# The input projection u @ w_in by Strassen's algorithm, ahead of the merges

## The chip, the cores and the metric

The kernel runs on one core of one Trainium2 chip. The metric is the device time of one launch in microseconds (us). Engines are named as the profile names them: PE (TensorE, matrix products), PEld (its weight loads), DVE (VectorE), ACT (ScalarE), POOL (GpSimd) and SP (SyncE, which here only issues DMAs). Each engine takes its instructions strictly in order; semaphores tie the engines together.

## What is computed

One layer with 1024 tokens and 1024 channels, in float32, cut to what matters:

```python
u = layer_norm(x) * (1 + scale) + shift              # shift, scale, gate from silu(c) @ w_ada + b_ada
proj = u @ w_in + b_in                               # w_in: 1024 x 12288
a_v, a_g, b_b, b_c, b_h, b_g, c_a, c_b, c_g, merge = split(proj)   # 1024 each, merge 3 x 1024
y_a = grouped_linear(causal_pool(a_v), pool_w) * pool_scale * silu(a_g)   # windows 2, 4, 8, 16
y_b = b_b * causal_dwconv3(b_c * b_h) * silu(b_g)
h_c = causal_dwconv31(c_a * sigmoid(c_b))
y_c = silu(layer_norm(h_c)) * silu(c_g)
m = sum_k sigmoid(merge_k) * (y_k @ w_branch[k])
out = layer_norm(ALPHA * x + gate * (m @ w_out))
```

## The kernel before

Channels lie on the 128 partitions and tokens on the free dimension, so blocks of weights are the stationary operand. float32 products are made of float32r parts: each operand is split into a high part (ACT, L97) and a low part (DVE subtracts, L98), and each product goes through PE in three passes (`mm3`, L100 to L103): low weights by high data, high by low, high by high.

The work is a list of jobs (`Job`, L260). A *projection job* takes one block of 128 columns of w_in: it loads 512 KB of raw weights on SP's queue, splits them in two pieces of 512, runs 8 k x 2 halves of the tokens x 3 passes = 48 matmuls of 128x512 into one PSUM tile of 1024 tokens, and then a function given to `proj` (L312) takes the result out of PSUM with its bias. There are 96 of them. A *z job* does the same with a column block of w_branch and the y of one branch (24 jobs); four *pool jobs* hold the grouped linear map. Loads are issued two jobs ahead, splits one job ahead.

The branches: `c_pair` (L345) makes the input of the 31-tap convolution, `conv_step` (L364) runs TAPS = 4 of its taps on DVE after each job, `a_v`, `a_g`, `a_pool` are branch A, `b_tile` branch B (four projections), the `c_` functions from L490 the layer norm of branch C. `merge` (L565) alternates a gate (a projection job with a sigmoid) and a z job, so all gates stay in SBUF only shortly, and y0, y1, y2 are kept split in SBUF. The convolution's outputs go to DRAM (h_dram) and come back (hc).

A hand-written list, START, sets the order of the first 80 us: statistics of x, the modulation sums, transposes, the pieces of u (`ul`, `uh`) and the products of the first three jobs as the pieces arrive. After that the jobs run in the order of the list, and a scheduler places each engine's instructions. Buffers: a pool of 44 tiles of 128 x 1024 (4 KB per partition) for everything large, two raw weight buffers, four buffers for split weights of 512 columns, and three PSUM tiles of 1024.

Of the kernel before, what the change touches and what calls it, by code (L numbers as in the profile page):

```python
# [35 lines left out]
BIG_SLOTS = 44  # L36
RAW_BUFS = 2
SPLIT_BUFS = 4
TAPS = 4
OUT_PARTS = (2, 2, 2, 2, 2, 2, 2, 4)  # L40
PAIR_EVERY = 6
C_STAGE = 4
C_YS = (0, 1, 2, 2, 3, 3, 4, 4)
# [5 lines left out]
def kernel(  # L49
# [26 lines left out]
    def main_ps(name):  # L76
        return ps_main.tile([P, D], F32, tag="main", name=name)
# [9 lines left out]
    def after(late, early):  # L87
        """Keeps the scheduler from issuing a load, and taking its slot, ahead of time."""
# [11 lines left out]
    def mm3(ps, wh, wl, rh, rl, start, stop):  # L100
        nc.tensor.matmul(ps, wl, rh, start=start, stop=False)  # L101
        nc.tensor.matmul(ps, wh, rl, start=False, stop=False)  # L102
        nc.tensor.matmul(ps, wh, rh, start=False, stop=stop)  # L103

# [18 lines left out]
    def columns(name, parts, q, cols=None):  # L123
        """Vectors of DRAM, each as columns of 128 channels."""
# [22 lines left out]
    u_hi = [slot(f"uh{k}", F32R) for k in range(NT)]  # L147
    u_lo = [slot(f"ul{k}", F32R) for k in range(NT)]
# [50 lines left out]
    def ada_sum(k):  # L199
        """c_act times the rows of w_ada; partition p of each part sums the rows p of some tiles."""  # L200
# [59 lines left out]
    class Job:  # L260
# [304 lines left out]
    def merge(b, AHEAD=2):  # L565
# [27 lines left out]
        for d in range(AHEAD):  # L593
            gate(d)
# [236 lines left out]
```

## Time and profile before

| what | value |
|---|---|
| median of 3 runs | 1480.46 us (1479.98 to 1480.49) |
| span of the profiled execution | 1479.1 us |
| PE busy | 1456.3 us, 98% |
| DVE busy | 851.8 us, 58% |
| ACT busy | 361.7 us, 24% |
| POOL busy | 27.2 us, 2% |
| moved by DMA | 104.53 MB, 71 GB/s |

The profiled execution has no time of its own beside its span; the span stands 1.4 us under the median of the runs, which were taken without a profile. A row of a group reads: line, engine, operation, output<-inputs by the program's names, shapes, count, then busy us and mean ns of one, then idle time of that engine just before and what ended it. A matmul is listed with its own latency, which is longer than the distance between two, since they are pipelined.

### The profile page before, as it was taken

The page shows a single profiled execution, that of the slowest core. Times are in us where ns is not written, and L with a number is a line of the kernel's source. Part 1 is how long each engine was busy: PE and PEld are TensorE (multiplying, and loading weights), DVE is VectorE, ACT ScalarE, POOL GpSimd, SP SyncE. Part 2 cuts the span into 40 slices and gives each one's busy share as a digit, 9 for nine tenths or more (in the row PEclk, how much of TensorE's full clock was granted, in tenths as well). Part 3 has the DMA queues.
Part 4 walks back from the last instruction along what each step waited for, and adds up shares of the span by engine and source line. Part 5 has one row for each costly group of instructions (what it writes and reads, how often), then busy time and mean ns, then how long its engine had stood idle before and what let it go on. Part 6 is the DMA issues. An engine that isn't in the chain of part 4 may idle for free.

```text
span 1479.1 us, 15467 instructions
## 1 busy us (share of the span) xinstructions
PE 1456.3 (98%) x6505; PEld 1208.2 (82%) x6505; DVE 851.8 (58%) x977; ACT 361.7 (24%) x478; POOL 27.2 (2%) x63
## 2 busy tenths in 40 slices
PE   7899999999999999999999999999999999999997
PEld 6788878888888888888888888888888888888887
DVE  6669999989393764939632332312224566322676
ACT  5433222222211112121221222211112346212300
POOL 1100000000000000000000000000000000000010
PEclk9999999999999999999999999999999999999999
DMA  9513322121212111121111111211114111112422
GB/s 306 134 29 100 108 71 65 43 64 43 72 43 66 49 58 57 43 68 47 57 57 43 46 55 43 58 43 43 57 43 163 51 43 43 57 43 66 162 100 86
DMA packets 152903, 104.53 MB, mean 71 GB/s; under 512 B 3844, under 2 KB 144208, under 8 KB 152832
## 3 DMA queue, kind: packets, MB, share of 16 engines
q1 hardware_dynamic: 150992, 98.06, 22.3%
q0 software_dynamic: 1792, 5.46, 1.1%
q8 instruction: 51, 0.84, 0.2%
q14 instruction: 20, 0.16, 0.0%
q10 hardware_dynamic: 48, 0.01, 0.0%
HBM read 95.12 MB, written 8.39 MB: 70 GB/s over the span
## 4 chain that ended last, share of the span: by engine, by line
PE 96%; SPq 3%; DMA 0%; DVE 0%; issue 0%; ACT 0%; DVEq 0%
PE ps_p L102 23%; PE ps_p L103 23%; PE ps_p L101 23%; PE ps_z L101 6%; PE ps_z L102 6%; PE ps_z L103 6%; SPq L191 2%; PE out_ps L101 2%; PE out_ps L103 2%; PE out_ps L102 2%; SPq L168 1%; PE pool_ps L103 0%; PE pool_ps L102 0%; PE pool_ps L101 0%; DMA raw_p<-in_w_in_dram 0%; PE tr L240 0%
## 5 line engine op out<-in xcount | busy, mean ns | idle before, releaser
L102 PE MATMUL ps_p<-ul,w_p 128*128 128x512 f32 x1536 | 599.5, 390 | 0.4 <-DVE ul L257 0.4
L103 PE MATMUL ps_p<-uh,w_p 128*128 128x512 f32 x1536 | 599.1, 390 | 0.0
L101 PE MATMUL ps_p<-uh,w_p 128*128 128x512 f32 x1536 | 596.9, 391 | 0.2 <-DVE w_p L98 0.2
L101 PEld LDWEIGHTS ps_p<-uh,w_p 128*128 128x128 f32 x1536 | 288.6, 188 | 61.6 <-issue 0.9
L102 PEld LDWEIGHTS ps_p<-ul,w_p 128*128 128x128 f32 x1536 | 289.3, 188 | 60.7 <-DVE ul L257 0.9
L103 PEld LDWEIGHTS ps_p<-uh,w_p 128*128 128x128 f32 x1536 | 289.2, 188 | 60.1
L373 DVE SCALAR_TENSOR_TENSOR h<-cs,cfw_cols,h 128x1023 f32<-128x1023 f32 (+14 forms) x240 | 303.7, 1266 | 7.9 <-ACT h L371 4.0
L98 DVE TENSOR_TENSOR w_p<-raw_p,w_p 128x512 fp32r<-128x512 f32 x192 | 131.5, 687 | 237.0 <-ACT w_p L97 236.8
L97 ACT ACTIVATE w_p<-raw_p 128x512 fp32r<-128x512 f32 x192 | 120.3, 629 | 488.0 <-PE ps_p L103 354.1
L98 DVE TENSOR_TENSOR w_z<-raw_z,w_z 128x512 fp32r<-128x512 f32 x48 | 33.0, 688 | 78.7 <-ACT w_z L97 78.7
L97 ACT ACTIVATE w_z<-raw_z 128x512 fp32r<-128x512 f32 x48 | 30.3, 631 | 157.2 <-PE ps_z L103 129.6
L580 DVE TENSOR_TENSOR g<-ps_z,g 128x1024 f32<-128x1024 f32 x24 | 29.4, 1224 | 68.0 <-PE ps_z L103 68.0
L573 ACT ACTIVATE g<-ps_p,bin_cols 128x1024 f32<-128x1024 f32 x24 | 26.8, 1115 | 100.7 <-PE ps_p L103 100.7
L324 DVE SCALAR_TENSOR_TENSOR bg<-ps_p,bin_cols,bg 128x1024 f32<-128x1024 f32 x8 | 10.3, 1282 | 31.2 <-ACT bg L323 31.1
L459 DVE SCALAR_TENSOR_TENSOR bc<-ps_p,bin_cols,bc 128x1024 f32<-128x1024 f32 x8 | 10.3, 1284 | 24.7 <-PE ps_p L103 24.7
L474 DVE SCALAR_TENSOR_TENSOR ba<-ps_p,bin_cols,ba 128x1024 f32<-128x1024 f32 x8 | 10.3, 1284 | 22.5 <-PE ps_p L103 22.5
L467 DVE SCALAR_TENSOR_TENSOR ba<-bc,vec_cols,ba 128x1023 f32<-128x1023 f32 (+1 forms) x16 | 20.5, 1281 | 4.5 <-ACT ba L463 4.3
L781 DVE TENSOR_TENSOR og<-out_ps,gate_b 128x512 f32<-128x512 f32 (+1 forms) x18 | 11.2, 629 | 19.9 <-PE out_ps L103 19.9
L356 DVE SCALAR_TENSOR_TENSOR cs<-ps_p,bin_cols,cs 128x1024 f32<-128x1024 f32 x8 | 10.3, 1281 | 20.7 <-PE ps_p L103 20.7
L324 DVE SCALAR_TENSOR_TENSOR cg<-ps_p,bin_cols,cg 128x1024 f32<-128x1024 f32 x8 | 10.2, 1281 | 19.2 <-ACT cg L323 19.2
L584 DVE TENSOR_TENSOR g<-g,g 128x1024 f32<-128x1024 f32 x16 | 19.5, 1218 | 0.0
L228 PE MATMUL mod<-c_act,ada 128*128 128x1 f32 x64 | 14.0, 352 | 5.2 <-DMA ada<-in_w_ada_dram 5.2
(452 smaller groups left out, 1536.3 us busy)
## 6 DMA issues: line engine op xcount, KB each, us to landing
raw_p<-in_w_in_dram SPq DMA_DIRECT2D x96, 512.0 KB, 3.9
raw_z<-in_w_branch_dram SPq DMA_DIRECT2D x24, 512.0 KB, 3.6
ada<-in_w_ada_dram SPq DMA_DIRECT2D x32, 256.0 KB, 6.4
x<-in_x_dram SPq DMA_DIRECT2D x8, 512.0 KB, 6.2
rawg<-in_w_ada_dram SPq DMA_DIRECT2D x8, 512.0 KB, 3.7
h_dram<-h POOLq DMA_DIRECT2D x8, 512.0 KB, 3.3
hc<-h_dram SPq DMA_DIRECT2D x8, 512.0 KB, 6.9
rawo<-in_w_out_dram SPq DMA_DIRECT2D x8, 512.0 KB, 3.7
```

The costliest lines, as they stand in the source:

```text
L97: nc.scalar.activation(hi, src, AF.Identity)
L98: marks["split"] = nc.vector.tensor_tensor(out=lo, in0=src, in1=f32(hi), op=ALU.subtract)
L101: nc.tensor.matmul(ps, wl, rh, start=start, stop=False)
L102: nc.tensor.matmul(ps, wh, rl, start=False, stop=False)
L103: nc.tensor.matmul(ps, wh, rh, start=False, stop=stop)
L191: nc.sync.dma_start(out=t[:, s], in_=ada_src[:, s, 4 * q : 4 * q + 4, k * P : (k + 1) * P])
L324: nc.vector.scalar_tensor_tensor(out=t, in0=ps, scalar=bias(col), in1=t, op0=ALU.add, op1=ALU.mult)
L373: nc.vector.scalar_tensor_tensor(out=h[:, s:], in0=g[:, : S - s], scalar=w, in1=h[:, s:], op0=ALU.mult, op1=ALU.add,)
L467: nc.vector.scalar_tensor_tensor(out=a[:, s:], in0=g[:, : S - s], scalar=vec("sc_w", (2 - s) * NT + ct), in1=a[:, s:], op0=ALU.mult, op1=A ...
L573: marks["u_done"] = nc.scalar.activation(gates[d], ps, AF.Sigmoid, bias=bias(col))
L580: nc.vector.tensor_mul(g, ps, g)
L584: marks["z"] = nc.vector.tensor_add(m[d], m[d], g)
```

## The change

All of u @ w_in but four column blocks is computed by Strassen's algorithm in its form with seven products. w_in's rows are cut into even and odd blocks k, and two column blocks form a *pair*; u is cut likewise into even and odd blocks and into the two halves of the tokens. So a pair is a 2x2 by 2x2 product of quarters: A11, A12 (first column block, even and odd rows), A22 (second column block, odd rows) and the sums S1 to S4 on the weights' side; B11, B21, B22 and the sums T1 to T4 on u's side. Each of the seven products is 4 blocks x 3 passes = 12 matmuls of 128x512.

- `sum_u` makes the sums of u once, after the start: 16 subtractions in place on DVE (L276 to L279) and eight splits of 1024.
- `Pair.prepare` makes S1 to S4 (four DVE instructions of 512, L368 to L372) and splits wa = the first raw block, wb = S1 and S2, wc = S3 and S4 (1024 each) and wd = A22 (512).
- `Pair.run` accumulates in two PSUM banks, which are read between products (ACT, L396, L398, L400), and puts the rest together by three DVE additions (L403, L405, L407).
- The functions that follow are rewritten for pairs (`c_pair`, `a_pair`, `b_first`, `b_second`, `gates`). Gates, y1, the silus of a_g and c_g, the pooled tiles and the centred convolution are stored in DRAM by POOL's queue (`store`) and loaded again (`y_load`, `a_load`, `c_square`, `c_y`, the g of `merge`).
- All pairs come first (4 ordinary jobs, then 46 pairs); then the z jobs of branch B with the pool jobs between them, then those of A, then of C. No gate is made between z jobs.
- TAPS is 6, then 5. Big tiles 44 to 37, raw buffers 2 to 4, split buffers 3 of 1024 columns, and six PSUM banks of 512 instead of three tiles of 1024. Silu is used as one function of ACT where the kernel before used Sigmoid and a multiplication.

```diff
-BIG_SLOTS = 44
-RAW_BUFS = 2
-SPLIT_BUFS = 4
-TAPS = 4
+BIG_SLOTS = 37
+RAW_BUFS = 4
+W8_BUFS = 3
+TAPS = 6
+TAPS_LATE = 5
+CLASSIC = 4
...
+    def sum_u(i):
+        even, odd = ut[2 * i], ut[2 * i + 1]
+        b11, b12, b21, b22 = even[:, LEFT], even[:, RIGHT], odd[:, LEFT], odd[:, RIGHT]
+        nc.vector.tensor_sub(b11, b12, b11)
+        nc.vector.tensor_sub(b12, b22, b12)
+        nc.vector.tensor_sub(b22, b22, b11)
+        nc.vector.tensor_sub(b21, b21, b22)
+        for n, t in ((0, even), (1, odd)):
+            hi, lo = slot(f"t{i}_{n}h", F32R), slot(f"t{i}_{n}l", F32R)
+            split(hi, lo, t)
+            sums[i, n] = hi, lo
...
+    class Pair:
+        def prepare(self):
...
+            wa = split8(f"wa_{self.name}", raw1)
+            nc.vector.tensor_add(s1, a2[:, 0], a2[:, 1])
+            nc.vector.tensor_sub(s2, s1, a1[:, 0])
+            wb = split8(f"wb_{self.name}", s12.rearrange("p n c -> p (n c)"))
+            nc.vector.tensor_sub(s3, a1[:, 0], a2[:, 0])
+            nc.vector.tensor_sub(s4, a1[:, 1], s2)
+            wc = split8(f"wc_{self.name}", s34.rearrange("p n c -> p (n c)"))
+            wd = wlast.tile([P, 2, HALF], F32R, tag="last", name=f"wd_{self.name}")
...
+        def product(self, ps, left, right, first):
+            w, block = self.left[left]
+            for i in range(4):
+                ks = slice(block(i) * P, (block(i) + 1) * P)
+                rh, rl = quarter(right, i)
+                mm3(ps, w[:, 0, ks], w[:, 1, ks], rh, rl, first and i == 0, i == 3)
+
+        def run(self):
...
+            self.product(px, "A11", "B11", True)
+            nc.scalar.activation(r1[:, LEFT], px, AF.Identity, bias=bias(col1))
+            self.product(pz, "S1", "T1", True)
+            nc.scalar.activation(r2[:, RIGHT], pz, AF.Identity, bias=bias(col2))
+            self.product(px, "S2", "T2", False)
+            nc.scalar.activation(r1[:, RIGHT], px, AF.Identity, bias=bias(col1))
+            py = bank(f"py_{self.name}")
+            self.product(py, "A12", "B21", True)
+            nc.vector.tensor_add(r1[:, LEFT], py, r1[:, LEFT])
+            self.product(px, "S3", "T3", False)
+            nc.vector.tensor_add(r2[:, RIGHT], px, r2[:, RIGHT])
+            self.product(pz, "S4", "B22", False)
+            nc.vector.tensor_add(r1[:, RIGHT], pz, r1[:, RIGHT])
+            self.product(px, "A22", "T4", False)
+            self.after(r1, px, r2)
...
+    def func(t, ps, f, col):
+        nc.scalar.activation(t[:, LEFT], ps, f, bias=bias(col))
+        nc.scalar.activation(t[:, RIGHT], t[:, RIGHT], f)
...
+    def y_load(b, k, mark):
+        t = slot(f"y{b}_{k}")
+        after(nc.sync.dma_start(out=t, in_=y_dram[b][k]), marks[mark])
+        y[b, k] = split_slots(f"y{b}_{k}", t)
...
+    def ahead(i):
+        for n, have, f in ((i + 2, loaded, "load"), (i + 1, prepared, "prepare")):
...
+        if i == n_proj - 1:
+            for k in range(NT):
+                y_load(1, k, "late")
```

The written order shows where this puts the work. First DVE, early among the projections. Before, between the low parts of two jobs' weights (w_p6272 in two pieces, then the first of w_p384), there are taps of the convolution (L373), a sum of the gate row (L700) and branch A's work:

```order
L98 TENSOR_TENSOR w_p6272_0_1137<-raw_p6272_1055,w_p6272_0_1137 128x512
L700 SCALAR_TENSOR_TENSOR gacc_1053<-rawg1_1132,c_act_117,gacc_1053 128x1024
L373 SCALAR_TENSOR_TENSOR h0_773<-cs0_768,cfw_cols_756,h0_773 128x1007
L373 SCALAR_TENSOR_TENSOR h0_773<-cs0_768,cfw_cols_756,h0_773 128x1006
L406 TENSOR_TENSOR s2_1_1114<-v2_1112 128x1023
L98 TENSOR_TENSOR w_p6272_512_1140<-raw_p6272_1055,w_p6272_512_1140 128x512
L373 SCALAR_TENSOR_TENSOR h0_773<-cs0_768,cfw_cols_756,h0_773 128x1005
L406 TENSOR_TENSOR s2_2_1117<-s2_1_1114 128x1022
L373 SCALAR_TENSOR_TENSOR h0_773<-cs0_768,cfw_cols_756,h0_773 128x1004
L98 TENSOR_TENSOR w_p384_0_1204<-raw_p384_1135,w_p384_0_1204 128x512
```

After, in the middle of pair d2 (branch B's second pair of tile 2), with the weights of cg2 (gates of branch C) being prepared and b2 being finished:

```order
L403 TENSOR_TENSOR r1_d2_2067<-py_d2_2108,r1_d2_2067 128x512
L112 TENSOR_TENSOR wa_cg2_2049<-raw_cg2_0_1910,wa_cg2_2049 128x1024
L477 SCALAR_TENSOR_TENSOR h2_2165<-r1_c2_1674,cfw_cols_836,h2_2165 128x1019
L564 SCALAR_TENSOR_TENSOR r2_b2_1935<-r1_b2_1934,vec_cols_832,r2_b2_1935 128x1023
L407 TENSOR_TENSOR r1_d2_2067<-pz_d2_2066,r1_d2_2067 128x512
L112 TENSOR_TENSOR wb_cg2_2054<-s12_cg2_2047,wb_cg2_2054 128x1024
L477 SCALAR_TENSOR_TENSOR h2_2165<-r1_c2_1674,cfw_cols_836,h2_2165 128x1018
L405 TENSOR_TENSOR r2_d2_2068<-px_d2_2065,r2_d2_2068 128x512
L564 SCALAR_TENSOR_TENSOR r2_b2_1935<-r1_b2_1934,vec_cols_832,r2_b2_1935 128x1022
L809 SCALAR_TENSOR_TENSOR gacc_1648<-rawg4_2173,c_act_123,gacc_1648 128x1024
L112 TENSOR_TENSOR wc_cg2_2059<-s34_cg2_2048,wc_cg2_2059 128x1024
L368 TENSOR_TENSOR s12_b3_2180<-raw_b3_1_2045 128x512
```

The low parts of the weights have become 1024 wide, and between them stand the sums of quarters and the additions that read PSUM (py, pz, px).

Second SP, at the passage to a merge. Before, in the approach to the third merge, the loads of the convolution's outputs (hc) stand together between raw weights of projection jobs:

```order
L507 DMA hc0_6993<-h_dram0_136 128x1024 [waits DMASW1_49,PE_49]
L274 DMA raw_p8704_7084<-in_w_in_dram 128x8x128 [waits DMAHW0_49,DVE_49]
L507 DMA hc1_6998<-h_dram1_137 128x1024 [waits DMASW4_49,PE_49]
L507 DMA hc2_7004<-h_dram2_138 128x1024 [waits DMASW7_49,DMASW5_49,DMASW0_49]
L507 DMA hc3_7006<-h_dram3_139 128x1024 [waits DMASW6_49,PE_49]
```

After, at the first merge, raw weights of z and pool jobs stand between loads of the tiles that these same jobs read (raw weights wait for DVE, whose split frees the buffer):

```order
L674 DMA y1_7_7014<-y1_dram7_149 128x1024 [waits DMAHW0_49,PE_49]
L525 DMA pool0_7020<-pool_dram0_158 128x1024 [waits DMAHW1_49,DMASW2_49,PE_49]
L300 DMA raw_pool3_7412<-in_pool_w_dram 128x2x256 [waits DMAHW2_49,DVE_49]
L528 DMA sga0_7026<-sga_dram0_166 128x1024 [waits DMAHW3_49,PE_49]
L525 DMA pool1_7028<-pool_dram1_159 128x1024 [waits DMASW5_49,DMASW4_49,DMAHW4_49,DMASW2_49,DMASW1_49]
...
L300 DMA raw_z1_5_7558<-in_w_branch_dram 128x8x128 [waits DMAHW4_49,DVE_49]
L626 DMA hc4_7161<-h_dram4_130 128x1024 [waits DMAHW5_49]
L626 DMA hc5_7168<-h_dram5_131 128x1024 [waits DMAHW6_49]
L525 DMA pool2_7175<-pool_dram2_160 128x1024 [waits DMAHW7_49,PE_49]
```

What moved is what the jobs of a merge read: it was in SBUF as it was made, and now comes through SP's queue, behind raw weights of later jobs.

More of the change, by code (lines that the diff above doesn't have):

```diff
@@ L334, with store, dram_tiles @@
+    def store(dst, src):
+        return nc.gpsimd.dma_start(out=dst, in_=src)
+    def dram_tiles(name, n):
+        return [dram.tile([P, S], F32, name=f"{name}{j}") for j in range(n)]
+    jobs = []
     hooks = {}
@@ new lines, in y_load, with merge, done @@
+    def y_load(b, k, mark):
+        t = slot(f"y{b}_{k}")
+        after(nc.sync.dma_start(out=t, in_=y_dram[b][k]), marks[mark])
+        y[b, k] = split_slots(f"y{b}_{k}", t)
+    def merge(b, first):
+        def z(d):
+            def done(ps):
+                g = slot(f"g{b}_{d}")
+                after(nc.sync.dma_start(out=g, in_=g_dram[b][d]), marks["late"])
+                for h in range(2):
+                    nc.vector.tensor_mul(g[:, HALVES[h]], ps[h], g[:, HALVES[h]])
+                if first:
@@ L609 @@
-    merge(0)
-    for ct in range(NT):
-        b_tile(ct)
-    rest = jobs[n_first:]
-    del jobs[n_first:]
-    j = 1
-    for i, job in enumerate(rest):
-        jobs.append(job)
-        if i % PAIR_EVERY == PAIR_EVERY - 1 and j < NT:
+    for j in range(CLASSIC // 2):
+        c_classic(j)
+    todo = []
+    for j in range(NT):
+        todo.append([lambda j=j: b_first(j), lambda j=j: b_second(j)])
+    for j in range(NT):
+        todo.append([lambda j=j: a_pair(j)])
+    light = [lambda i=i: gates(f"cg{i}", C_CG + 2 * i * P, AF.Silu, sgc_dram[2 * i : 2 * i + 2]) for i in range(NT // 2)]
@@ new lines @@
+    for b in (1, 0, 2):
+        for i in range(NT // 2):
+            light.append(
+                lambda b=b, i=i: gates(
+                    f"m{b}_{i}", C_M + b * D + 2 * i * P, AF.Sigmoid, g_dram[b][2 * i : 2 * i + 2]
+                )
+            )
+    heavy = [f for group in todo for f in group]
+    heavy_n, light_n = len(heavy), len(light)
+    order, li = [], 0
+    for n, f in enumerate(heavy):
+        order.append(f)
+        while li < (n + 1) * (light_n - 2) // heavy_n:
+            order.append(light[li])
+            li += 1
@@ L618 @@
+    order += light[li:]
+    every = 6
+    j = CLASSIC // 2
+    for n, f in enumerate(order):
+        if n % every == every - 1 and j < NT:
             c_pair(j)
             j += 1
+        f()
     assert j == NT
-    n_b = len(jobs)
-    merge(1)
-    n_c = len(jobs)
-    for ct in range(NT):
-        c_g(ct)
-    merge(2)
-    for j in range(NT):
-        hook(n_c, c_load, j)
-        hook(n_c + j // 2, c_square, j)
-    hook(n_c + C_STAGE, c_rstd)
-    hook(n_c + C_STAGE + 1, c_spread)
@@ L644 @@
         else:
-            jobs[n].load(first=True)
+            jobs[n].load()
     n_first = 0
@@ L653 @@
             elif what == "s":
[L654 removed]
+                jobs[at[0]].prepare()
                 n_first = at[0] + 1
```

435 lines of the change are left out of this document (227 added, 208 removed).

## The prediction

> **What bounds the kernel now.** I read the page's span, the busy times and the chain that ended last first, then the waits of TensorE, then the groups, and last single stretches of the windows and the timeline.
>
> ```profile
> span 1479.1 us, 15467 instructions
> PE 1456.3 (98%) x6505; PEld 1208.2 (82%) x6505; DVE 851.8 (58%) x977; ACT 361.7 (24%) x478; POOL 27.2 (2%) x63
> PE 96%; SPq 3%; DMA 0%; DVE 0%; issue 0%; ACT 0%; DVEq 0%
> ```
>
> TensorE is busy in 98% of the span and is 96% of the chain. It idles 22.8 us in all, and the longest waits that TensorE has on anything are these (columns: total, times, longest), all in the first 55 us:
>
> ```profile
> PE mod L228 <- DMA ada<-in_w_ada_dram: 5.2, 2, 3.9
> PE tr L240 <- ACT ut L246: 4.3, 1, 4.3
> PE ps_p L102 <- DVE ul L257: 0.4, 1, 0.4
> ```
>
> So between the start and the tail nothing is ever waited for: time is matmuls times their pitch. The pitch comes from a stretch in which TensorE is busy throughout (columns: PE, PEld, DVE, ACT, POOL busy with counts, granted clock, DMA share, GB/s):
>
> ```profile
> 200.00:400.00 200.00, 200.00 (x884) 165.59 (x883) 164.46 (x164) 49.16 (x75) 2.12 (x4) 1.00 0.19 56
> ```
>
> 200.00/884 = 0.2262 us per matmul, at full clock. In the same stretch DVE is busy 164.46 of 200, so it is not idle where the projections run: it is the second resource, and the change loads it. The prices of DVE and ACT that I need:
>
> ```profile
> L98 DVE TENSOR_TENSOR w_p<-raw_p,w_p 128x512 fp32r<-128x512 f32 x192 | 131.5, 687 | 237.0 <-ACT w_p L97 236.8
> L97 ACT ACTIVATE w_p<-raw_p 128x512 fp32r<-128x512 f32 x192 | 120.3, 629 | 488.0 <-PE ps_p L103 354.1
> L781 DVE TENSOR_TENSOR og<-out_ps,gate_b 128x512 f32<-128x512 f32 x14 | 9.6, 688 | 17.1 <-PE out_ps L103 17.1
> 195.19 1.21 DVE L98 TENSOR_TENSOR ya2l<-sga,ya2h 128x1024 fp32r<-128x1024 f32 x1
> 196.32 1.26 DVE L373 SCALAR_TENSOR_TENSOR h<-cs,cfw_cols,h 128x1011 f32<-128x1011 f32 x1
> 197.50 1.21 DVE L98 TENSOR_TENSOR ya3l<-sga,ya3h 128x1024 fp32r<-128x1024 f32 x1
> 198.64 1.26 DVE L373 SCALAR_TENSOR_TENSOR h<-cs,cfw_cols,h 128x1010 f32<-128x1010 f32 x1
> L97 ACT ACTIVATE yc0h<-hc 128x1024 fp32r<-128x1024 f32 x1 | 1.1, 1063 | 0.6 <-DVE hc L552 0.6
> L140 ACT ACT_TABLE_LOAD x1 | 1.3, 1283 | 1.7 <-PEq L818 1.7
> ```
>
> The timeline's starts show that back to back a 1024-wide subtraction takes 1.14 us (197.50 to 198.64) and a tap 1.18 (196.32 to 197.50), some 0.07 under the listed durations; I take the 512-wide one at 0.61. An operand in PSUM costs DVE no more (688 against 687).
>
> **The change, part by part.**
>
> *Products.* Before, 96 column blocks take 48 matmuls each. After, 92 of them go as 46 pairs of 84 (7 products of 4 blocks by 3 passes) and 4 stay at 48: 4056 for 4608, 552 fewer. At 0.2262 that is **-124.9 us**, on the chain in full as long as TensorE stays fed: a floor of 1354.2. A pair is 19.0 us of TensorE.
>
> *DVE beside the pairs.* A pair has three 1024-wide low parts and one of 512 (3 x 1.14 + 0.61 = 4.0), four sums of quarters (4 x 0.61 = 2.4) and three additions out of PSUM (1.8): 8.3 us, where the same two blocks had four 512-wide low parts, 2.4. Six taps add 7.1, where two jobs had eight. That leaves 3.6 us for what follows a pair: 0 after gates, 1.1 after a C pair, 2.3 after the second B pair, 3.5 after the first, 2.3 to 6.9 after an A pair (its widest windows have four additions, a scaled one and two tiny ones). Adding up the rows of the written order between successive first additions (L403), each at its pitch, gives 745 us of DVE for 45 pairs, against 855 of TensorE: 87%. The first sixteen stand at 96%, and some are over: up to 22.5 against 19.0, beside others of 9 to 14. So on average TensorE is still the slower, with locally up to 3.5 us of lag, which the neighbours give back. What such a lag does: the order on TensorE puts the next pair's A11, S1 and part of A12 between S3·T3 and A22·T4, so the addition at L405 has 5.4 us or more before TensorE misses it, while the ones at L403 and L407 hold nothing soon. ACT's evictions (0.63 each) have 2.7 us between S2·T2 and S3·T3. I take **+10** for the projections; the ends are 0 (every lag is covered) and 70 (the heavy pairs' excess of 1.5 us in each of 46).
>
> *ACT.* Its row is 24% now. A pair puts 3 x 1.06 + 0.63 of high parts, 3 x 0.63 of evictions and 1 to 2.5 of functions on it, under 9 of 19.0 us. Silu beside Sigmoid brings 26 more table loads, 26 x 1.28 = 33 us spread out; ACT's slack hides it: 0.
>
> *DRAM.* Eighty more stores and about as many loads of 512 KB are 84 MB. The two bursts of before:
>
> ```profile
> 1135.00:1140.00 5.00, 5.00 (x24) 4.14 (x23) 1.83 (x2) 0.76 (x2) 0.00 (x0) 1.00 1.03 386
> 1140.00:1145.00 5.00, 5.00 (x24) 4.14 (x23) 3.87 (x5) 3.65 (x4) 0.00 (x0) 1.00 1.02 406
> raw_z<-in_w_branch_dram SPq DMA_DIRECT2D x24, 512.0 KB, 3.6
> h_dram<-h POOLq DMA_DIRECT2D x8, 512.0 KB, 3.3
> ```
>
> At some 396 GB/s a tile takes 1.32 us, TensorE's pitch does not change in them (24 matmuls in 5 us), and the mean rate only rises from 71 towards 130 GB/s. Bandwidth costs 0; the order of the loads is what costs, below.
>
> *The start.* Sixteen subtractions (L276 to L279), eight low parts of the sums and the first pair's own 8.3 us less its additions come onto DVE just where the rows of u are made, while job 3 is not prepared until after them:
>
> ```profile
> 72.00:76.00 4.00, 4.00 (x19) 3.30 (x18) 0.74 (x2) 0.00 (x0) 0.00 (x0) 1.00 0.00 0
> 76.00:80.00 4.00, 4.00 (x21) 3.27 (x20) 0.95 (x2) 1.41 (x2) 0.00 (x0) 1.00 0.00 0
> 78.81 0.69 DVE L257 TENSOR_TENSOR ul<-ut,uh 128x512 fp32r<-128x512 f32 x1 [6.04 <-ACT uh L254]
> ```
>
> In these rows TensorE never idles though the last piece of u comes at 78.81: jobs 3 and 4 fill it. After, only jobs 0 to 2 are ready; behind the last piece of u stand two subtractions, four low parts and job 3's own (2 x 0.61 + 5 x 1.14 = 6.9 us). Taking the last piece some 2.5 us sooner, since less stands ahead of it on TensorE, job 3 starts near 83, and some 57 of the matmuls done by then before, 13 us, are still to do: **+13**, ends 6 (PE finds the pieces sooner) and 20.
>
> *The first merge.* This is the largest loss. SP issues in order, and a load of raw weights waits there for its buffer, that is for a split, that for one of three weight buffers, and that for the product that frees it. Among these now stand the loads of y, pool, sga, h and g:
>
> - y1_0 stands behind raw_z1_3, which waits for w_z1_1's split, which waits for the last pair's wc (S3·T3). From there 2.2 (split: 1.06 + 1.14), 3.6 (landing) and 2.2 (y's own split) against 2.7 of A22·T4: 5.3, and 0.9 at A22·T4 itself, which here has no next pair to cover it.
> - pool1 stands behind raw_pool3, that behind w_pool1's split, that behind the end of z1_0: 2.2 + 3.6 + 2.2 = 8.0 less some 2 of products on pool0: 6.
> - pool2 and pool3 stand behind raw_z1_5, which waits for the end of z1_1, with five tiles ahead (about 6 us): 2.2 + 6 + 3.6 + 2.2 = 14 less 5.4 of pool1 and what z1_2 lacks: 10. The last squares, var and rstd come behind raw_z1_6 and raw_z1_7 alike: 10. One more at pool3.
>
> Together **+34**. The lower end is 0 (SP runs far enough ahead); the upper 56, seven waits of the full 8.0.
>
> *The clock.* What an idle TensorE meets:
>
> ```profile
> 52.63 1.97 PE L240 MATMUL tr<-ident,x 128*128 128x128 f32 x8 [4.33 <-ACT ut L246]
> 52.00:54.00 2.00, 1.37 (x7) 1.37 (x8) 2.00 (x6) 2.00 (x4) 0.00 (x0) 0.50 0.05 14
> 54.00:56.00 2.00, 2.00 (x7) 1.71 (x6) 2.00 (x5) 2.00 (x5) 0.18 (x1) 0.50 0.89 259
> 56.00:58.00 2.00, 2.00 (x6) 1.51 (x6) 2.00 (x6) 1.58 (x4) 2.00 (x4) 0.50 0.54 151
> ```
>
> After 4.33 us of idling the granted clock is 0.50 until 58: 5.4 us at half speed, 2.7 lost. Four gaps of the merge are that long: 11 at most, and 0 if they stay shorter; part is lost in waits that come anyway, so I take **+7**. The Trainium skill, in "TensorE: Matmul & The Clock Gate", section "Part 1: The HAM clock gate (the "warmup" mystery)", says that an idle window of about 3.4 us halves the clock and that about 3.4 us of work brings it back. By that the four gaps would cost 4 x 1.7 = 6.8, an estimate from that page; the trace agrees with the halving and shows the return later, after 5.4 us, and the row decides.
>
> *The other merges and the tail.* z0 and z2 find y behind raw loads in the same way, but nothing short stands between their jobs: **+3** (0 to 10). The products with w_out are the same; 0, with 4 either way since loads and slots there moved.
>
> Sum: 1479.1 - 124.9 + 10 + 13 + 34 + 7 + 3 = 1421.2. The profiled span lies 1.4 under the median 1480.46, so I forecast **1422 us**.
>
> **Rivals.**
>
> 1. *DVE sets the pace of the projections.* For it: the 96% of the first sixteen pairs, and DVE's 82% of before in 200 to 400 us. Against it: 87% over all, and covers of 2.7 to 5.4 us. With 0.6 to 1.2 us lost per pair beyond my 10: 1450 to 1477.
> 2. *The loads of the merge are hidden.* Landing 3.6 us and four raw buffers may suffice, and a scheduler that places work by readiness fills the start; then -124.9 with 10 to 40 us of stalls: 1366 to 1395. Against it: the chain raw buffer, split, weight buffer, product is closed in the written order, and the jobs between are short (5.4 us for a pool job).
> 3. *The slots run out, slower than before.* The big pool falls from 44 to 37 tiles; 28 hold u and its sums, and 9 are left for r1 and r2 of two pairs, g, h and the running sum of the convolution, B's kept tile and the gate row. A new r1 then waits until a store has left (3.3 us to land, and 88 stores share POOL's queue), so ACT's eviction at L396 waits, holds its PSUM bank, and everything behind it on ACT. If an eviction comes 1.3 us too late in each of 46 pairs, that is 60 us and all is lost; a full landing less the cover, 3.3 - 2.7 = 0.6, falls short of it, which speaks against this, two store landings (3.9) would exceed it: 1483 to 1560.
>
> **How the numbers follow.** A measurement of this kernel cannot tell 0.2% (3 us) from nothing. My case, 1395 to 1447, has 0.58; rival 1 0.19; rival 2 0.14; rival 3 0.07; 0.02 is left between, within 0.2%. Faster is 0.58 + 0.19 + 0.14 = 0.91. The range leaves out rival 3, the upper part of rival 1 and the lowest part of rival 2: 1378 to 1468.
>
> **What would show it.** After: 5736 wide matmuls at the same 0.226 pitch in the projections, so about 19 us from pair to pair; DVE near 90% busy there and 80% over all; TensorE's waits no longer a few lines of the start but waits on DVE's y and pool low parts at the first merge, about 34 us in some six gaps, with the granted clock at 0.50 behind the longer ones; a gap of about 13 us near 75 to 90 us. I am wrong if TensorE waits in the projections on DVE (px or the weights' low parts) by more than 25 us, if waits on ACT's evictions behind stores show up, or if the first merge has no gaps.

## The result, and the profile after

The changed kernel takes **1447.97 us**, the median of four runs (1444.24 to 1449.66), against 1480.47 of the kernel before on the same chip: a ratio of 0.9777, 95% interval 0.9763 to 0.9791. I had forecast 1422 (1378 to 1468). The profiled execution itself took 1444.24 with a span of 1442.4; its terms are worked out below against that span, and the median lies 3.7 above its time.

The page of the kernel after: span, busy times of the engines and the chain that ended last.

```profile
span 1442.4 us, 15371 instructions
PE 1352.8 (94%) x5953; PEld 1114.4 (77%) x5953; DVE 1091.3 (76%) x1296; ACT 526.0 (36%) x649; POOL 68.8 (5%) x143
PE 82%; DMA 6%; issue 4%; DVE 3%; SPq 3%; ACT 2%; POOL 0%; DVEq 0%; ACTq 0%; POOLq 0%
```

TensorE has 552 matmuls fewer, as counted, but 94% busy for 98%, and its share of the chain falls from 96% to 82%. Its waits (total, times, longest) no longer lie in the first 55 us alone (three rows of the start, 6.2 and 5.4 on loads of parameters and 3.1 on high parts of u, are left out):

```profile
PE pool_ps L116 <- ACT pool2h L111: 15.6, 1, 15.6
PE rstd_ps L655 <- DVE diag L654: 6.8, 1, 6.8
PE mod L240 <- ACT ut L257: 5.5, 1, 5.5
PE ps_z L116 <- ACT y_0h L111: 4.9, 1, 4.9
PE px_a L116 <- DVE wa_a L112: 3.5, 1, 3.5
PE px_m L116 <- ACT r_m L396: 3.4, 2, 1.8
PE cfw_ps L149 <- DVE vec_cols L150: 3.2, 1, 3.2
PE px_d L116 <- DVE wa_d L112: 3.1, 1, 3.1
PE var_ps L640 <- DVE sq L634: 2.9, 1, 2.9
PE px_m L116 <- DVE wa_m L112: 2.5, 1, 2.5
PE pool_ps L116 <- ACT pool1h L111: 2.4, 1, 2.4
PE pool_ps L116 <- ACT pool0h L111: 1.7, 1, 1.7
```

Where the loss sits is read from two stretches of the windows (columns as in the prediction), the 46 pairs and the first merge:

```profile
104.00:1003.00 899.00, 884.28 (x3873) 727.72 (x3871) 774.05 (x847) 377.20 (x484) 34.59 (x65) 1.00 0.30 95
1005.00:1105.00 100.00, 65.25 (x248) 50.45 (x247) 51.37 (x59) 28.71 (x30) 9.17 (x15) 0.78 0.78 286
```

In the second, 248 matmuls would take 56.1 us at 0.2262; 43.9 of the 100 us are lost. The six waits that lie in it (y_0h, pool0h, pool1h, pool2h, sq, diag) make 34.3 of that. TensorE is busy 65.25 us with work of 56.1, so 9.2 of the remaining 9.6 are matmuls at a lower clock: the mean granted clock there is 0.78.

The start is compared by matmuls in the first 100 us: windows of the kernel before for its three lines of products, then of the kernel after for its one.

```profile
0.00:100.00 100.00, 28.00 (x75) 14.41 (x75) 0.97 0.62 168
0.00:100.00 100.00, 30.68 (x74) 15.05 (x75) 0.97 0.62 168
0.00:100.00 100.00, 30.26 (x74) 14.76 (x74) 0.97 0.62 168
0.00:100.00 100.00, 45.72 (x163) 32.35 (x164) 0.91 0.66 181
```

Before, 223 are done, after 163: 60 x 0.2262 = 13.6 us are still to do. The timeline shows the pace of the pairs by the first and the last of 46 first additions:

```profile
118.09 0.69 DVE L403 TENSOR_TENSOR r_b<-py_b,r_b 128x512 f32<-128x512 f32 x1
993.18 0.69 DVE L403 TENSOR_TENSOR r_m<-py_m,r_m 128x512 f32<-128x512 f32 x1 [2.90 <-PE py_m L116]
```

That is 875.09 / 45 = 19.45 us from pair to pair, 0.45 over the 19.0 of TensorE: 20.7 us in 46.

The end: the drain of POOL's queue at the last instructions (views of that source line, before and then after; ns shortest/median/longest).

```profile
L827 POOLq DRAIN  x3: 46/93/2752, 1473.6 to 1478.9; - x3
L953 POOLq DRAIN  x3: 46/93/9287, 1432.3 to 1442.1; - x3
```

The longest drain grows from 2.75 to 9.29 us, and from the last matmul to the end of the span it is now 12.3 us for 7.5: 4.8 more.

All together: 1442.4 lies 88.2 above the floor of 1354.2. Start 13.6, pairs 20.7, first merge 43.9 and end 4.8 make 83.0; 5.2 are left for the other merges and the rest. The forecast had 67.

### The profile page after: what moved, and what is told of

Same layout as the page of the kernel before. It is cut to its first block, busy times and chain, and to the rows that moved or that the text cites. A ratio compares the mean times of both kernels' runs of the same rounds, so it can differ in the third digit from the quotient of the medians.

```text
span 1442.4 us, 15371 instructions
## 1 busy us (share of the span) xinstructions
PE 1352.8 (94%) x5953; PEld 1114.4 (77%) x5953; DVE 1091.3 (76%) x1296; ACT 526.0 (36%) x649; POOL 68.8 (5%) x143
## 4 chain that ended last, share of the span: by engine, by line
PE 82%; DMA 6%; issue 4%; DVE 3%; SPq 3%; ACT 2%; POOL 0%; DVEq 0%; ACTq 0%; POOLq 0%
PE ps_z L116 13%; PE px_m L116 9%; PE px_a L116 6%; PE px_d L116 6%; PE px_b L116 6%; PE out_ps L116 6%; PE pz_m L116 4%; PE px_c L116 4%; PE pz_a L116 3%; PE px_cg L116 3%; PE pz_d L116 3%; PE pz_b L116 3%; PE ps_p L116 2%; PE pz_c L116 2%; PE py_m L116 2%
## 5 line engine op out<-in xcount | busy, mean ns | idle before, releaser
L477 DVE SCALAR_TENSOR_TENSOR h<-r_c,cfw_cols,h 128x1023 f32<-128x1023 f32 (+9 forms) x180 | 227.4, 1263 | 5.0 <-ACT h L475 4.4
L477 DVE SCALAR_TENSOR_TENSOR h<-cs,cfw_cols,h 128x1023 f32<-128x1023 f32 (+29 forms) x60 | 75.8, 1264 | 2.2 <-ACT h L475 1.7
L111 ACT ACTIVATE w_z<-raw_z 128x1024 fp32r<-128x1024 f32 x24 | 25.3, 1058 | 113.9 <-PE ps_z L116 93.4
L116 PE MATMUL ps_p<-u,w_p 128*128 128x512 f32 x192 | 52.6, 425 | 3.5 <-ACT u L265 3.1
L116 PEld LDWEIGHTS ps_p<-u,w_p 128*128 128x128 f32 x192 | 37.7, 205 | 12.6 <-ACT u L265 4.0
L116 PE MATMUL ps_z<-y_0h,w_z 128*128 128x512 f32 x96 | 35.4, 403 | 4.9 <-ACT y_0h L111 4.9
L116 PE MATMUL px_m<-u,wa_m 128*128 128x512 f32 x144 | 34.7, 390 | 2.5 <-DVE wa_m L112 2.5
L116 PE MATMUL py_m<-u,wa_m 128*128 128x512 f32 x144 | 35.9, 389 | 0.0
L116 PE MATMUL ps_z<-y_3h,w_z 128*128 128x512 f32 x96 | 34.1, 391 | 1.1 <-ACT y_3h L111 1.1
L116 PE MATMUL pz_m<-u,wc_m 128*128 128x512 f32 x144 | 35.1, 389 | 0.0
L116 PE MATMUL ps_z<-y_1h,w_z 128*128 128x512 f32 x96 | 34.4, 394 | 0.0
```

The lines of the kernel that those rows point to most:

```text
L111: nc.scalar.activation(hi, src, AF.Identity)
L116: nc.tensor.matmul(ps, w, r, start=start and n == 0, stop=stop and n == 2, skip_group_check=True)
L477: nc.vector.scalar_tensor_tensor(out=h[:, s:], in0=g[:, : S - s], scalar=w, in1=h[:, s:], op0=ALU.mult, op1=ALU.add,)
```

## The experiments

All edits are to the kernel after, except where another one is named. Theory and rivals stand in each expectation.

**Eight products instead of seven.** Same order, stores, loads and buffers, but each pair as two plain column blocks of 48 matmuls, without sums.

```diff
-            self.product(px, "A11", "B11", True)
-            self.product(pz, "S1", "T1", True)
...
+            for n, (t, h, col) in enumerate(((r1, 0, col1), (r1, 1, col1), (r2, 1, col2), (r2, 0, col2))):
+                ps = bank(f"p{n}_{self.name}")
+                self.product(ps, self.w[n // 2], h)
```

> The changed kernel with the seven products of a pair replaced by the plain eight: each pair runs 96 matmuls (two column blocks, two halves of the tokens), no sums of quarters, no sums of u. Everything else stays: all projections first, gates and branch outputs through DRAM, the order of the jobs, the buffers. Theory (the first merge loses about 43 us because its loads stand behind raw weights on SP, whatever the projections are made of; the end loses 4 to 5): 6288 wide matmuls as before, 1480.5 + 43 + 5, so 1518 to 1535 us, with the waits on pool2h, pool1h, y_0h and diag still there. Rival (the merge is late because the pairs leave DVE behind): the waits at the merge shrink below 20 us and the time is 1480 to 1500.

Measured: 1541.84 us in one run, beside 1480.52 of the kernel before, and more than the 1518 to 1535 expected. The new order and the stores cost 61 us, and the algorithm itself gives 1541.84 - 1447.97 = 93.9 back out of 124.9. The waits of TensorE in the merge are there without Strassen, while the stretch of the projections loses nothing (its window):

```profile
PE pool_ps L116 <- ACT pool2h L111: 18.2, 1, 18.2
PE rstd_ps L623 <- DVE diag L622: 6.8, 1, 6.8
```

```profile
104.00:1003.00 899.00, 899.00 (x3963) 743.21 (x3962) 461.97 (x391) 276.91 (x349) 29.43 (x56) 1.00 0.27 84
```

The kernel before does the same 3963 matmuls in that window. In the first 100 us this kernel does 394 matmuls of all kinds, the kernel before 400 and the kernel after 340. So the merge's loss belongs to the new order with its stores and loads, and the 31 us missing from the algorithm lie where its sums are made, at the start and in the pairs (13.6 and 20.7 above).

**The stores alone**, in the kernel before: eighty stores of 512 KB on POOL's queue.

```diff
+    scratch = [dram.tile([P, S], F32, name=f"scratch{j}") for j in range(80)]
...
+        if 10 <= i < 90:
+            nc.gpsimd.dma_start(out=scratch[i - 10], in_=f32(u_lo[i % NT]))
```

> The kernel before, with 80 more stores of 512 KB from POOL's queue (low parts of u into DRAM tiles that nobody reads), one per job from job 10 to 89, and nothing else. Theory (POOL's last drain takes longer the more DMAs it has issued, and the end waits for it): that drain grows from 2.75 us to about 9, the last matmul still ends some 8 us earlier than that, and the time is +4 to +6, 1485 us; the projections' pitch stays 0.226. Rival (the longer end of the changed kernel comes from something else): drain 3 us, 1480.5 plus or minus 1.

Measured: 1538.26 us in one run. As a price of stores it failed: nothing held them back, so the scheduler put them at the start, from 34 us on, where POOL also makes the powers of the statistics, and TensorE's longest wait there is new.

```profile
PE tr L240 <- ACT ut L246: 24.9, 1, 24.9
```

One part is answered: the last drain of POOL's queue is 9.29 us in it too, with 101 DMAs issued on that queue as in the kernel after, for 21 before. The longer end comes from POOL's DMAs and not from the products.

**The pool jobs two z jobs later**, which gives the loads of the pool tiles more time.

```diff
+    jobs += z_jobs[:2]
     for g in range(4):
-        jobs.append(z_jobs[g])
+        jobs.append(z_jobs[g + 2])
         a_pool(g)
-    jobs += z_jobs[4:]
+    jobs += z_jobs[6:]
```

> The changed kernel with one edit: the pool jobs stand two z jobs later (z1_0, z1_1, z1_2, pool0, z1_3, pool1, z1_4, pool2, z1_5, pool3, z1_6, z1_7); the places in the loop where pool tiles are loaded stay. Theory (order of issue against the short jobs' cover): every pool tile has 21.7 us more before it is needed, the waits on pool0h, pool1h and pool2h (19.7 us in the changed kernel) and most of those around var and rstd go, the clock stays up, and the time falls by 20 to 35 us, to 1413 to 1428. Rival (the stretch is bound by bandwidth, 344 GB/s at a DMA share of 0.94 in the longest gap): as many bytes have to come through, the gap only moves, and the time falls by less than 8.

Measured: 1452.13 us (four runs, ratio 0.9815 [0.9797, 0.9832]), not below the 1447.97 of the kernel after. TensorE's long wait moved to the squares, 25.3 us. SP's waits, and then a stretch ahead of that wait in the windows, show what came before it:

```profile
SPq L300 <- DVE w_pool L112: 37.0, 2, 29.6
```

```profile
1026.00:1044.00 18.00, 18.00 (x81) 14.89 (x81) 0.03 (x1) 0.63 (x1) 0.00 (x0) 1.00 0.00 0
```

For 18 us, while TensorE still has work, the DMA share is 0.00 although the squares' loads are due: SP stands before a raw_pool load whose buffer is not free, and the others stand behind it. That is the queue of the prediction, seen directly. The rival's number came true, the gap only moved, but not its reason: the DMA engines stood idle ahead of it.

**The loads of y, pool, sga and h on POOL's queue**, out of SP's way.

```diff
-            after(nc.sync.dma_start(out=t, in_=pool_dram[ct]), marks["late"])
+            after(nc.gpsimd.dma_start(out=t, in_=pool_dram[ct]), marks["late"])
...
```

> The changed kernel with the loads of the first merge (y1, pool, sga, the eight hc) issued by POOL's queue, so that none of them stands behind a load of raw weights; the order of the jobs is unchanged. Theory (SP's order): the wait on pool2h falls from 15.6 to under 5, those on pool1h and the last squares shrink, -12 to -30 us, 1418 to 1436. Rival (bandwidth, or free tiles, hold the loads): the waits stay within 5 us of what they were and the time is 1443 to 1453.

Measured: 1475.03 us (six runs, 0.9962 [0.9947, 0.9977]), 27 us more than after. In the waits, TensorE on pool2h and POOL's own queue:

```profile
PE pool_ps L116 <- ACT pool2h L111: 39.3, 1, 39.3
POOL c_dram L412 <- DVE hc L627: 42.6, 8, 9.0
```

The loads left one queue in which they stand behind raw weights for another in which they stand behind stores, and these wait for DVE to centre hc.

**Raw loads held back.** The raw weights of a z or pool job are issued only after a mark that an earlier job sets, so that SP reaches the other loads first.

```diff
...
                     getattr(jobs[at], f)()
+                    if f == "load" and at >= n_proj + 2:
+                        after(jobs[at].loaded, marks["ran"])
```

> The changed kernel with one edit: from the third z or pool job on, the load of a job's raw weights is held in the written order until the job two before it has taken its product out of PSUM, so that on SP the loads of pool, sga, hc, nc and sgc stand ahead of raw weights whose buffers are not free yet. Job order unchanged. The two runs before this one left both theories open: in the run with later pool jobs DMA moved nothing for 18 us (share 0.00 from 1026 to 1044) while SP stood 29.6 us before one raw_pool. Theory (SP's head of line): pool2h, sq and diag waits fall from 25 us together to under 10, the first merge loses under 25 us instead of 46, 1418 to 1432 us. Rival (tiles of the big pool are not free earlier, so the loads wait for those instead): waits move to other tiles, 1440 to 1455.

Measured: 1434.72 us (four runs, 0.9691 [0.9675, 0.9707]), 13 less than after. But TensorE still waits for pool2h, 14.4 us, and SP's waits tell why: it no longer waits for raw buffers there, but for tiles that are still being read, by the products of a pool job or by a store.

```profile
SPq L528 <- PE pool_ps L116: 12.2, 3, 8.7
SPq L528 <- DMA c_dram<-hc: 10.6, 1, 10.6
```

With two more rows (6.8 and 5.7), 23.1 us of SP's waits there are for stores of the centred convolution (c_dram). Theory and rival are both right in part: mending the queue's order wins 13 us, and behind it stand tiles that are not free; what the store of the centred convolution costs is tried below.

**Both, raw loads held and pool jobs later:**

> The same edit together with the later pool jobs (z1_0, z1_1, z1_2, pool0, z1_3, pool1, ...). Theory (SP's head of line): now the longer cover is usable, the waits at the merge go to y_0h and little else, the loss under 15 us, 1408 to 1425 us. Rival (free tiles, or bandwidth): no better than the run with the raw loads held alone, or than 1440.

Measured: 1443.66 us (four runs, 0.9747 [0.9727, 0.9767]), 9 more than with the loads held alone; now the weights come late (`ps_z` waits 12.7 us for w_z, `pool_ps` 9.9 for w_pool). The rival's number holds, but not its reason: what is late is neither tiles nor bytes but weights that were held back too long.

**Two buffers for A22**, since the one of `wlast` makes each pair's last split wait for the product before.

```diff
-BIG_SLOTS = 37
+BIG_SLOTS = 38
...
-            wd = wlast.tile([P, 2, HALF], F32R, tag="last", name=f"wd_{self.name}")
+            wd = pair_slot(f"wd_{self.name}")
```

> The changed kernel with the split A22 quarter (wd) taken from the big pool, which gets one tile more (38), in place of its single buffer: the same memory, but the next pair's wd needn't wait until A22·T4 of this pair has run. In the changed kernel DVE waits 61 us in the projections for ACT's wd, ACT for the product before it, and TensorE misses wa behind that in three places (3.1, 2.5, 3.5 us, each with half clock after it). Theory (the single buffer holds ACT and DVE in line): those three waits and most of the others between 104 and 1003 us go, the pairs' mean distance falls from 19.45 to 19.15 us or less, -8 to -16 us, 1432 to 1440. Rival (DVE's own load, 774 of 899 us, makes the lag): the waits stay, 1445 to 1450.

Measured: 1447.42 us (four runs, 0.978 [0.9765, 0.9794]): no change. DVE's waits for wd's high parts fell from 63.8 to 6.3 us in all, and the pairs' stretch from 899.0 to 897.2. The rival's time holds, though not its sign that the waits stay: TensorE's waits on wa_d and wa_m are gone, and others on ACT's evictions have come in their place (r_b 2.9, r_d 2.9 for 1.5, r_m 3.8 for 3.4). Freeing one buffer moved the waits and left their sum nearly as it was, and most of the 63.8 us that DVE waited were no loss, since nobody waited for DVE.

**The start rearranged**: job 3 is prepared ahead of the sums of u, and the first pair's sums wait until the pieces of u have been split.

```diff
+    jobs[3].load()
+    jobs[3].prepare()
...
     for i in range(NT // 2):
         sum_u(i)
...
+            if self.name == "b0":
+                for ins in (s1_ins, s3_ins, marks["hi"], marks["split"]):
+                    after(ins, marks["u", 3])
```

> The changed kernel with the start's order mended in two ways: the sums and the A22 split of the first pair are held until the fourth row block of u is split (they wait for a load that lands at 54 us, and ACT's and DVE's work on u stands behind them), and the splits of u's sums are held until the weights of job 3 are split and the parameter columns copied. Theory (both queues' order makes the start's 13.8 us): the waits on ut at 55.8 us (5.5), vec_cols and bin_cols (5.0) and the half clock behind them go, -6 to -12 us, 1436 to 1442. Rival (the 19 us of added DVE work must be done by then in any order): the wait moves to the first pair's S1·T1 and the time stays within 3 us of 1447.

Measured: 1442.54 us (four runs, 0.975 [0.973, 0.977]), between theory and rival. By 60 us the profiled execution, the slowest of the four with 1447.06, has done 85 wide matmuls for 57, but at 120 us 254 for 251: the 6 us won are given back in one wait of 7.6 on ACT's `cs`. That is what the rival says of the start, so the median's 5 us less are not found there, and their cause stays open. The wait on pool2h, whose code nobody changed, was 15.6 us in the kernel after, 18.5 with two buffers for A22, 23.0 here and 23.1 with a third of the taps, so a few us between such kernels can come from there.

**No store of the centred convolution**, added to the held loads: hc is squared in place, and h is loaded a second time and the mean subtracted again.

```diff
-        store(c_dram[j], t)
-        sq = slot(f"sq{j}")
+        sq = t
...
-        after(nc.sync.dma_start(out=n, in_=c_dram[ct]), marks["spread"])
+        after(nc.sync.dma_start(out=n, in_=h_dram[ct]), marks["spread"])
+        nc.vector.tensor_sub(n, n, c_state["mean"])
```

> The kernel of e5_raw_held with one edit more: the centred convolution isn't stored and loaded again. hc is squared in place, which frees its tile without a store, and the last stage loads the convolution's output itself and subtracts the mean a second time (eight more DVE subtractions of 1.14 us). In e5_raw_held SP still waits 23 us at the first merge for tiles that the stores of hc hold, with a DMA share of 0.92 to 1.08 in most slices. Theory (what is left of the merge's loss after SP's order is free tiles and bytes, both of which this eases: 4 MB and eight held tiles fewer): the wait on pool2h falls from 14.4 to under 8, 1420 to 1430 us. Rival (something else holds pool2, or the bytes of the rest alone fill the stretch): 1432 to 1438.

Measured: 1422.35 us (four runs, 0.961 [0.9595, 0.9626]), 12 less than the held loads alone. The wait on pool2h is gone; what follows it are weights that now come too late, in TensorE's waits:

```profile
PE ps_z L116 <- DVE w_z L112: 8.1, 2, 4.9
PE pool_ps L116 <- DVE w_pool L112: 4.9, 1, 4.9
```

**A third of the taps**: the convolution makes 10 of its taps after the first, two per job, and leaves the rest out.

```diff
-            if s == K31 - 1:
+            if s == 10:
...
-            conv_step(TAPS if i < n_proj else TAPS_LATE)
+            conv_step(2 if i < n_proj else 2)
```

> The changed kernel with a third of the convolution: each of the eight tiles runs 10 taps after its first in place of 30 (the others are left out), two per job, so that DVE has some 160 x 1.18 = 190 us less to do during the projections. Theory (DVE's load makes the 25 us that the projections lose: heavy pairs of 20 to 22 us): the waits on wa_d, wa_m, wa_a and on r_m, r_d disappear, the pairs' mean distance falls from 19.45 to 19.1, about -12 to -18 us, 1430 to 1437. Rival (the losses come from the order in which ACT and DVE serve a pair, whatever their load): the same waits in the same places, at most 5 us gained in the projections.

Measured: 1432.7 us in one run. DVE's busy time falls by 176 us in the window of the pairs (which here takes in the first 7 us behind them):

```profile
104.00:1003.00 899.00, 886.28 (x3888) 729.74 (x3887) 598.16 (x689) 380.39 (x488) 35.11 (x66) 1.00 0.31 97
```

The pairs themselves, from first to last matmul, shrink from 899.0 to 889.4 us, 19.30 from pair to pair; in the kernels with all taps they took from 897 to 904, and 914 in the one with all mends together (below). The waits on wa_d and wa_a are gone; wa_m (2.5), r_m (3.1) and r_d (1.5) remain. So some 10 of the 20.7 us hang on DVE's load, and what remains is something else, the evictions on ACT among it.

**Together**: held loads, no centred copy, another rearrangement of the start, and 32 DMAs of 512 bytes on POOL's queue, which bring its count to 125.

> The mends together: e9_no_centred_copy; the start of e8_start, with the splits of u's sums now held until ACT has taken job 0 out of PSUM (that run gained 6 us up to 60 us and gave them back in a wait of 7.6 us on that eviction); and 32 DMAs of 512 bytes more on POOL's queue. The last is for POOL's final drain: it took 9.29 us in every kernel with 88 stores, but 2.67 in e4_load_queue, which has 32 DMAs more on that queue, so it is not the count that makes it long. Theory: first merge as in e9_no_centred_copy, start -6 to -9 us, end -4.4 us; in sum 1408 to 1422. If the drain stays at 9.29, the last term is missing; if the wait on ACT's eviction stays, the middle one.

Measured: 1445.65 us (five runs, 0.9764 [0.9751, 0.9777]); a miss. The drain did not shorten but grew to 11.25 us. The small DMAs went to the start, like the stores above, and TensorE waits there for what POOL then makes late; the rearranged start has a wait of its own, 8.7 us on ACT's first eviction of a pair:

```profile
PE tr L252 <- ACT x L194: 13.9, 3, 12.2
```

**The best**: no centred copy, raw loads held one job less far back, and 40 small DMAs held until the merges.

```diff
+                    if f == "load" and at >= n_proj + 2:
+                        after(jobs[at].loaded, rans[-2])
...
+        rans.append(marks.get("ran"))
+        if i == n_c + 2:
+            for n in range(40):
+                after(nc.gpsimd.dma_start(out=tiny[n : n + 1, :], in_=ones[0:1, :]), marks["z"])
```

> The kernel of e9_no_centred_copy with two edits. First, raw weights are held one job less long (until the job three before, not two, has left PSUM): in e9_no_centred_copy TensorE now waits for split weights themselves, 8.1 us on w_z and 4.9 on w_pool. Second, 40 DMAs of 512 bytes more on POOL's queue, late, where POOL has nothing to do (in e11_together 32 such stood ahead of the start and POOL's powers waited behind them). POOL's last drain was 2.75, 8.63, 9.29 and 11.25 us with 21, 93, 101 and 125 DMAs on its queue, 0.082 us each, but 2.67 with 133; this kernel has 133. Theory: the waits on w_z and w_pool fall under 5 us together, -8 to -13; if the one short drain came of passing 128 DMAs, it is under 3 us here and the end comes 4 us sooner: 1406 to 1415 in all. Rival: with raw loads back ahead of pool and hc the wait on pool2h returns (14 us), and a drain by count would be 11.9 us: 1425 to 1432.

Measured: **1408.04 us** (five runs, 0.9523 [0.951, 0.9536]), 40 under the kernel after, with a span of 1404.9. Its window of the first merge and its last drain:

```profile
1005.00:1105.00 100.00, 90.70 (x385) 73.14 (x384) 77.58 (x87) 38.96 (x41) 8.64 (x14) 0.93 0.92 331
```

```profile
L959 POOLq DRAIN  x3: 46/93/2019, 1399.4 to 1404.7; - x3
```

The merge does 385 matmuls for 248 in the same 100 us, 137 x 0.2262 = 31 us. The longest drain is 2.02 us, and from the last matmul to the end it is 7.7 for 12.3. The waits on w_z and w_pool are gone, and on pool2 2.3 us remain, so the rival is out. Start and pairs are as in the kernel after.

## Why the prediction was right, and where it was off

The kernel became faster by the mechanism forecast, but the saving of 32.5 us is little more than half of the 58.5 forecast.

- *Products, -124.9:* right. The count of matmuls is the one forecast, and pairs cost what their matmuls cost wherever TensorE is fed; the eight-product kernel gives the algorithm 93.9 us net of its own sums.
- *The start, +13:* 13.6, with a cause partly different, so that the size is partly luck. I had job 3 late near 83 us and one gap of about 13 us, which is not there. The timeline shows the loss earlier and later: ACT stands 9.34 us at a split and DVE 5.03 at a sum of the first pair, whose raw weights have not landed, with the pieces of u behind them, and TensorE idles 5.49 us where it was 4.33 before,

```profile
54.45 0.69 DVE L368 TENSOR_TENSOR s_b<-raw_b 128x512 f32<-128x512 f32 x1 [5.03 <-DMA raw_b<-in_w_in_dram]
55.80 0.37 PE L240 MATMUL mod<-ones,acc 128*128 128x1 f32 x1 [5.49 <-ACT ut L257]
```

  and near 90 us the transposes of parameter columns wait for DVE's copies (1.8 and the 3.2 on vec_cols), with half clock behind them from 90.3 to 97.1. That the size held all the same agrees with the rearranged start: there the work of DVE and ACT that is due by 120 us set it, not one wait.
- *Projections, +10:* the term that was most mis-sized, 20.7. The trace accounts for most of it: TensorE idles 14.7 us in the window (899.00 - 884.28), and half clock from 175.6 to 179.0 and from 912.9 to 916.3 costs 3.4 more. Of the idle time 9.1 are three waits on low parts of wa, where "the neighbours give back" failed; taking out 176 us of DVE's work removes two of the three, and wins 9.6. Another 4.9 are waits on ACT's evictions at L396 (r_m 3.4 and r_d 1.5), which remain with less work on DVE. These I had costed at nothing ("ACT's slack hides it"). The one at 504.04 us takes A11·B11 out of PSUM, a product that is done at 495.07, and TensorE runs 8.2 us of other products before it misses it. But ACT takes its queue in order, and ahead of that eviction stand a split that waits for the previous pair's last product, done at 500.28, and the first tap of a convolution, which waits for DVE:

```profile
502.89 1.24 ACT L475 ACTIVATE h<-r_c,vec_cols,cfw_cols 128x1024 f32<-128x1024 f32 x1 [1.32 <-DVE r_c L463]
```

  The same two stand ahead of the one at 775 us, and a split that waits for TensorE ahead of the one at 954 us. No store is among these, so rival 3, evictions behind stores, is not borne out. Rival 1 is right in its kind and refused in its size: it set 28 to 55 us above my sum, and the pairs took 10.7.
- *The first merge, +34:* 34.3 us of waits. The mechanism, loads behind raw weights on SP, is shown three times: by the 18 us without any DMA, by the 13 us that held loads win, and by what SP waits for between 990 and 1110 us in the kernel after, which are raw buffers (32.3 more on w_pool) and hardly anything else:

```profile
SPq L300 <- DVE w_z L112: 56.7, 5, 18.5
```

  But that the sum agrees is luck in part, for the terms (which add up to 33.2) do not: pool2 took 15.6 where I had 10, pool0 1.7 and pool1 2.4 where I had 6 for pool1, y_0h 4.9 where I had 6.2; var and diag with 2.9 + 6.8 come close to the 10 I had. What made pool2 longer is "bandwidth costs 0", a step that failed: the windows around that wait of the kernel after show the DMA engines full.

```profile
1050.00:1056.00 6.00, 0.00 (x0) 0.00 (x0) 4.19 (x4) 2.66 (x3) 1.06 (x2) 0.74 0.78 234
1056.00:1062.00 6.00, 0.00 (x0) 0.00 (x0) 3.51 (x3) 1.08 (x2) 0.53 (x1) 0.50 1.05 401
1062.00:1068.00 6.00, 2.55 (x6) 2.07 (x7) 4.80 (x5) 3.06 (x3) 0.53 (x1) 0.50 1.03 420
```

  The DMA issues of 1050 to 1070 us (KB each, median us from issue to landing) name what fills them:

```profile
c_dram<-hc POOLq DMA_DIRECT2D x4, 512.0 KB, 6.8
pool<-pool_dram SPq DMA_DIRECT2D x2, 512.0 KB, 9.1
g<-g_dram SPq DMA_DIRECT2D x1, 512.0 KB, 13.0
```

  The load of pool2 is issued at 1054.26, 4.4 us after TensorE has run dry, and lands 8.1 us later; another 3.1 pass until its high part is made. I had seen such bursts before the change, where nothing waited for them, and had reckoned 3.6 us for a landing, the price of raw_z. The same page had a price for eight tiles loaded in a burst, nearly twice that:

```profile
hc<-h_dram SPq DMA_DIRECT2D x8, 512.0 KB, 6.9
```

  Leaving out the stores of the centred convolution removes the wait on pool2h, and with the held loads alone it stays 14.4. So the loss is the queue's order and the tiles and transfers of c_dram together; whether tiles held by the store or its transfers weigh more was not separated. Rival 2, a merge without stalls, is refused.
- *The clock, +7, and the other merges, +3:* 9.6 and 5.2. The first is right in kind; of the five stretches at half clock two come behind gaps shorter than I thought (below). The second is what is left of the sum.
- *The end, 0:* 4.8. The tail's matmuls are the same, but I had not looked at what eighty more DMAs on POOL's queue do to its last drain.

Against the forecast of 67 over the floor the terms so measured stand 0.6 higher at the start, 10.7 in the pairs, 0.3 in the first merge's waits, 2.6 in the clock, 2.2 in the other merges and 4.8 at the end: the 21.2 us between 67 and 88.2. The pairs are half of it. My list of TensorE's waits before the change left out one of 5.1 us, on the columns of b_ada at the very start; it is 5.4 after and changes no term. DVE is busy 86% of the pairs' stretch and 76% over all, where I had said near 90% and 80%.

## What to carry to other kernels

A large saving on a saturated engine shows its price at the seams: cost each stage where the saved engine first runs out of prepared work, and follow every in-order queue there, with what stands ahead of each load and which tile it needs. A rate that was harmless while nobody waited (a full DMA, an 87% busy second engine) must be costed again at each place where the change makes somebody wait. And a value that is cheap to make again is better not stored: leaving out the centred copy won 12 us on top of the held loads, its second subtraction included.

## What the runs showed of the hardware

*The last drain of POOL's queue follows the number of DMAs issued on it.* With 21 it takes 2.75 us, with 93 8.63, with 101 9.29 in all nine such kernels, with 125 11.25: about 0.082 us for each. With 133, in two kernels, it is short again, 2.67 and 2.02. Why it falls there stays open; a multiple of 128 is a guess.

*Gaps below 3 us can halve the clock, and it matters when they come.* In the kernel after, the timeline and the windows behind two gaps of 1.73 and 2.43 us, and behind one of 2.46 us in the pairs:

```profile
1027.07 1.20 PE L116 MATMUL pool_ps<-pool0h,w_pool 128*128 128x512 f32 x4 [1.73 <-ACT pool0h L111]
1034.05 1.21 PE L116 MATMUL pool_ps<-pool1h,w_pool 128*128 128x512 f32 x4 [2.43 <-ACT pool1h L111]
```

```profile
1029.00:1031.00 2.00, 2.00 (x7) 1.52 (x5) 0.00 (x0) 0.00 (x0) 0.00 (x0) 0.50 1.00 369
1032.00:1034.00 2.00, 0.00 (x0) 0.00 (x0) 0.00 (x0) 1.06 (x1) 0.00 (x0) 0.91 1.01 383
1036.00:1038.00 2.00, 2.00 (x6) 1.60 (x5) 1.61 (x3) 0.00 (x0) 0.00 (x0) 0.50 0.52 211
640.80:642.80 2.00, 2.00 (x9) 1.66 (x10) 2.00 (x3) 0.96 (x2) 0.00 (x0) 1.00 0.37 108
```

The clock is 0.50 for 3.4 us after each of the first two, with the full clock between, and stays 1.00 after the third. Yet in the kernel without the centred copy the same wait of the same pair, 2.46 us again, is followed by half clock:

```profile
640.80:642.80 2.00, 2.00 (x5) 1.61 (x6) 2.00 (x3) 0.85 (x2) 0.00 (x0) 0.50 0.40 113
```

The records of the granted clock in the two traces show a difference. In each trace all changes of the clock lie on one raster with steps of 3.41 us (19 changes in each, within 0.01 us). In the kernel after, the gap from 638.33 to 640.79 is cut by the raster at 639.84, into 1.51 and 0.95 us; in the other kernel the gap from 638.22 to 640.68 is cut at 640.19, into 1.97 and 0.49, and at 640.19 the clock falls. So what one step of the raster holds of a gap seems to decide, and a few tenths of a us in when a wait comes change its price. How much it takes is not settled: 1.53 us in one step were enough behind the gap of 1.73, and a gap of 1.53 at 774 us, all in one step, was not. The Trainium skill, in "TensorE: Matmul & The Clock Gate", section "Part 1: The HAM clock gate (the "warmup" mystery)", sets the idle window at about 3.4 us; the step of the raster agrees with that length, but these rows do not bear out that TensorE has to idle for all of it, and they decide.
